# Gated linear attention in smaller tiles of the array: 64x64 score products masked in one pass, output products in column and quarter tiles

## The chip, the cores and the metric

The kernel runs on one core of a Trainium2 chip. The core has five engines, each with its own queue that is worked off in order: TensorE (PE; its weight loads are listed as PEld), VectorE (DVE), ScalarE (ACT), GpSimd (POOL) and SyncE (SP), which issues the DMAs. TensorE multiplies a stationary operand (the weights, up to 128 rows by 128 columns) with a moving operand of up to 512 columns and writes to PSUM, eight banks of 512 f32 values for each of 128 partitions. The metric is the device time of one execution in microseconds (us), lower is better.

## The reference

Two layers over 1024 tokens of width 1024. Each layer projects the normed input to a latent-attention group and to a gated linear attention (GLA) group, multiplies each branch with its gate, projects back, and adds a gated per-layer embedding. The change touches the GLA group: four heads, key width 64, value width 128, chunks of 64 tokens, run forward and backward with separate decays and summed.

```python
def gla_chunked(q, k, v, log_a):          # C = 64, N = S // C = 16 chunks
    b = jnp.cumsum(gc, axis=-2)
    ref = b[..., C // 2 - 1:C // 2, :]
    q_in = qc * jnp.exp(b - ref)
    k_in = kc * jnp.exp(ref - b)
    mask = jnp.tril(jnp.ones((C, C), dtype=bool))
    A = jnp.where(mask, jnp.einsum('nbhid,nbhjd->nbhij', q_in, k_in), 0.0)
    o_intra = jnp.einsum('nbhij,nbhjv->nbhiv', A, vc)
    ...
    def step(state, inp):
        qi, ki, vi, di = inp
        o = jnp.einsum('bhid,bhdv->bhiv', qi, state)
        state = state * di[..., None] + jnp.einsum('bhjd,bhjv->bhdv', ki, vi)
        return state, o
    _, o_inter = lax.scan(step, s0, (q_inter, k_state, vc, decay))
    o = o_intra + o_inter
# o = rmsnorm(gla_chunked(q, k, v, la_f) + flip(gla_chunked(flipped, la_b)), out_norm)
```

## The kernel before

Activations lie transposed, features on the partitions and 1024 tokens along the free axis. Large products split each f32 operand into a high and a low f32r part and add three products (`mm3`, line 162; weights are loaded and split in `load_split`, lines 140 to 142: a DMA, a ScalarE copy, a GpSimd subtraction). The GLA products take f32 operands as they are.

For one GLA head, partitions 0 to 63 hold the key features of the forward direction and 64 to 127 those of the backward one. `gla_decay` (step Z) computes the decays; it begins with a product into a PSUM tile (line 370) and ends with `qi`, `ki` and `qb`. `gla_state` (step S) transposes the keys (line 412), forms the per-chunk state updates (line 425, in two row tiles of 64 rows), copies them out of PSUM (line 104) and runs the scan over the chunks with 28 small VectorE instructions (line 452). It then computes the scores. For each of eight pairs of chunks t, and for each direction, one product of 64 rows takes the 128 tokens of the pair against the same 128 tokens (line 459), so that each product holds four 64x64 blocks, of which the two off the diagonal belong to no chunk. The forward scores go to one PSUM tile and the backward ones to another, each 128x1024. A mask that is zero off the diagonal blocks and triangular in them steers one VectorE pass for each direction (line 461) into `af` and `ab`, which were cleared once a layer; GpSimd adds the two (line 465) to `at`, whose off-diagonal blocks are zero. `gla_out` (step O) adds into one PSUM tile, for each chunk, state times `qb` (line 473: 128x128 weights, 64 moving columns), and for each pair of chunks values times `at` (line 477: 128x128 weights, 128 moving columns). ScalarE copies the result out and squares it (line 480), a norm follows, GpSimd multiplies by the gate, and a DMA writes the head out.

PSUM is held by two tags, `mm` and `aux`, with two buffers of two banks each. Line 370, the state updates, the scores, the output and the norms take `aux`; the big products mostly take `mm`. SBUF tiles of 128x1024 come from one ring of 41 buffers.

The order of the steps is written by hand in two strings, one a layer; within and across steps the program builder orders each engine's queue by a simulation of its own. In layer 0 the string's GLA part reads `K0 R0 Q0 G0+ Z0 V0 K1 S0 Z1 V1 O0 S1 Q1 D0 Z2 G1 G2 P0 O1 S2 ...`: the output of a head comes well after its scores, with other products between.

Of the kernel before, what the change touches and what calls it, by code (L numbers as in the profile page):

```python
# [10 lines left out]
F32 = mybir.dt.float32  # L11
F32R = mybir.dt.float32r
I32 = mybir.dt.int32
U32 = mybir.dt.uint32
AF = mybir.ActivationFunctionType
ALU = mybir.AluOpType
# [3 lines left out]
P = 128  # L20
# [3 lines left out]
HC = 512  # L24
EPS = 1e-6
NH = 4
CH = 64
# [24 lines left out]
ORDER = ("K0 R0 Q0 G0+ Z0 V0 K1 S0 Z1 V1 O0 S1 Q1 D0 Z2 G1 G2 P0 O1 S2 C0 Z3 D1 C1 N0 D2 O2 S3 G3 M0 A0 O3 X0 A1 E0 A2 A3+ H0 k0 T0 s0 v0 H2 k1+ s1 k2 b0 H1 k3 s2 y1 b1 H3+ s3 b2 v1 s4 y0 y3 b3 y2 s5 b4 w0 w1+ s6 w2 b5 w3+ s7 w4 b6 w5+ s8 w6 w7 b7",  # L52
         "Q0 K0 Z0 V0 S0 Z1 V1 S1 Q1 K1 Z2 G0 O0 S2 G1 Z3 G2+ C0 O1 D0 O2 S3 G3 C1 N0 D1 D2+ O3 M0 X0 A0 A1 E0 A2 k0 y2 H0 A3 T0 s0 v0 H3 k1+ s1 H1 b0 H2 s2 k2 b1 s3 y0 k3+ b2 v1 s4 y3 y1 b3 s5 b4 w0 w1+ s6 w2+ b5 w3 s7 w4 b6 w5+ s8 w6+ w7 b7")

ENG = dict(at="P", qi="V", qb="P", og="P", gate="P", sq="V", wlo="P", kT="A", put="A", o="A", ple="A", hadd="V")
TCKW = {"schedule_with_timeline_sim": True}


# [1 line left out]
def hybrid_encoder(ctx: ExitStack, tc: tile.TileContext, xT, pT, pos, vecs, w_in, wq, wk, wv,  # L60
                   wz, w_out, w_gate, w_proj, outT, dbg=None):
    nc = tc.nc
    dbg = dbg or {}

    cp = ctx.enter_context(tc.tile_pool(name="const", bufs=1))
# [13 lines left out]
    ones_r = cp.tile([P, P], F32R, name="ones_r")  # L79
    nc.vector.memset(ones_r.bitcast(F32), 1.0)  # L80

    mask_f = cp.tile([P, P], F32, name="mask_f")
    mask_b = cp.tile([P, P], F32, name="mask_b")
    for m, sgn in ((mask_f, 1), (mask_b, -1)):
        nc.vector.memset(m, 1.0)
        nc.vector.memset(m[0:CH, CH:P], 0.0)
        nc.vector.memset(m[CH:P, 0:CH], 0.0)
        nc.gpsimd.affine_select(out=m, in_=m, pattern=[[sgn, P]], compare_op=ALU.is_ge,
                                fill=0.0, base=0, channel_multiplier=-sgn)
    rmask = cp.tile([P, S], mybir.dt.bfloat16, name="rmask")  # L90
    nc.gpsimd.memset(rmask, 1.0)
    nc.gpsimd.memset(rmask.rearrange("p (n c) -> p n c", c=CH)[:, :, 0:1], 0.0)
# [3 lines left out]
    def bank2(tag="mm"):  # L96
        return pp.tile([P, 2, HC], F32, tag=tag, name="ps")

    def on(site):
        return {"P": nc.gpsimd, "V": nc.vector}[ENG[site]]  # L100

    def copy(site, dst, src):
        if ENG[site] == "A":
            nc.scalar.activation(dst, src, AF.Copy)  # L104
        else:
            nc.vector.tensor_copy(dst, src)
# [7 lines left out]
    def flat(t):  # L114
        return t.rearrange("p a b -> p (a b)")

    def st(shape=(P, S), dt=F32, name="st"):
        return sp.tile(list(shape), dt, tag="st", name=name)

    def mt(dt=F32, name="mt"):  # L120
        return rp.tile([P, S], dt, tag="r", name=name)
# [152 lines left out]
    sq = SquareSum()  # L274
# [8 lines left out]
    for L in range(DEPTH):  # L283
        vb = L * V_LAYER

        def gv(off, j):
            return vec[:, vb + off + j:vb + off + j + 1]
# [5 lines left out]
        rc = cp.tile([P, 8], F32, tag="rc", name="rc", bufs=2)  # L293
        r_x = rstd(sq.acc, D, col=rc)

        af, ab = mt(name="af"), mt(name="ab")
        for t in (af, ab):
            nc.gpsimd.memset(t, 0.0)
        wzr = st(name="wzr")[0:32, 0:HC]
        wzt = mt(F32R, name="wzt")[:, 0:HC]  # L300
        nc.sync.dma_start(wzr, wz[L])
# [104 lines left out]
        def gla_state(h, v, dec):  # L406

            qi, ki, qb, ks_, alpha = dec

            fp = flat(bank2("aux"))  # L410
            for t in range(8):
                nc.tensor.transpose(out=fp[:, t * P:(t + 1) * P], in_=ks_[:, t * P:(t + 1) * P], identity=ident)
            kT = mt(name="kT")
            copy("kT", kT, fp)
            kT = kT.rearrange("p (a b) -> p a b", b=P)

            s0, s1 = (mt(name=n).rearrange("p (n c) -> p n c", c=P) for n in ("s0", "s1"))
            nc.gpsimd.memset(s0[0:CH, 0, :], 0.0)
            nc.gpsimd.memset(s1[CH:P, 7, :], 0.0)
            for half in range(2):  # L420
                pu = bank2("aux")
                for j in range(8):
                    c = half * 8 + j
                    rows = slice((c % 2) * CH, (c % 2) * CH + CH)
                    nc.tensor.matmul(pu[:, j % 2, (j // 2) * P:(j // 2 + 1) * P], lhsT=kT[rows, c // 2, :],
                                     rhs=v[c // 2][rows], start=True, stop=True)

                u4 = pu.rearrange("p b (n c) -> p n b c", c=P)

                def put(dst, src):  # L430
                    copy("put", dst, src)

                if half == 0:
                    put(s0[0:CH, 1:7, :].rearrange("p (n b) c -> p n b c", b=2), u4[0:CH, 0:3])
                    put(s0[0:CH, 7, :], u4[0:CH, 3, 0, :])
                    put(s1[0:CH, 0, :], u4[0:CH, 3, 1, :])
                    put(s0[CH:P, 0, :], u4[CH:P, 0, 1, :])
                    put(s0[CH:P, 1:7, :].rearrange("p (n b) c -> p n b c", b=2), u4[CH:P, 1:4])
                else:
                    put(s1[CH:P, 1:7, :].rearrange("p (n b) c -> p n b c", b=2), u4[CH:P, 1:4])  # L440
                    put(s1[CH:P, 0, :], u4[CH:P, 0, 1, :])
                    put(s0[CH:P, 7, :], u4[CH:P, 0, 0, :])
                    put(s1[0:CH, 1:7, :].rearrange("p (n b) c -> p n b c", b=2), u4[0:CH, 0:3])
                    put(s1[0:CH, 7, :], u4[0:CH, 3, 0, :])

            def state(c):
                return (s0, s1)[c // 8][:, c % 8, :]

            for c in range(1, NCH - 1):
                e = NCH - 1 - c  # L450
                for rows, m, n in ((slice(0, CH), c, c + 1), (slice(CH, P), e, e - 1)):
                    nc.vector.scalar_tensor_tensor(state(n)[rows], state(m)[rows], alpha[rows, m:m + 1],  # L452
                                                   state(n)[rows], op0=ALU.mult, op1=ALU.add)

            blocks = [(af, slice(0, CH), mask_f, flat(bank2("aux"))), (ab, slice(CH, P), mask_b, flat(bank2("aux")))]
            for t in range(8):
                c = slice(t * P, (t + 1) * P)
                for acc, rows, mask, fa in blocks:
                    nc.tensor.matmul(fa[:, c], lhsT=ki[rows, c], rhs=qi[rows, c], start=True, stop=True)
            for acc, rows, mask, fa in blocks:  # L460
                nc.vector.copy_predicated(acc.rearrange("p (n c) -> p n c", c=P),
                                          mask.bitcast(U32).unsqueeze(1).to_broadcast((P, 8, P)),
                                          fa.rearrange("p (n c) -> p n c", c=P))
            at = mt(name="at")
            on("at").tensor_tensor(at, af, ab, op=ALU.add)
            return state, at

        def gla_out(h, v, qb, state, at, gg):

            fo = flat(bank2("aux"))  # L470
            for n in range(NCH):
                cc = slice(n * CH, (n + 1) * CH)
                nc.tensor.matmul(fo[:, cc], lhsT=state(n), rhs=qb[:, cc], start=(n % 8 == 0), stop=False)
                if n % 2:
                    t = n // 2
                    c = slice(t * P, (t + 1) * P)
                    nc.tensor.matmul(fo[:, c], lhsT=v[t], rhs=at[:, c], start=False, stop=(n % 8 == 7))
            o, o2 = mt(name="o"), mt(name="o2")
            copy("o", o, fo)
            nc.scalar.activation(o2, fo, AF.Square)  # L480
            r = rstd(o2, P, tmp=mt)
            nc.vector.scalar_tensor_tensor(o, o, gv(V_ON, 0), r, op0=ALU.mult, op1=ALU.mult)
            on("og").tensor_tensor(o, o, gg, op=ALU.mult)
            nc.sync.dma_start(ygd[h], o)
# [176 lines left out]
        def new_part():  # L661
            return (cp.tile([P, 4], F32, tag="top", name="top", bufs=3),
                    cp.tile([P, 4], F32, tag="sums", name="sums", bufs=4), [])
# [52 lines left out]
        for w in ORDER[L].split():  # L716
            u = int(w[1])
            other[0] = w.endswith("+")
            h, c = divmod(u, 2)
# [6 lines left out]
            elif w[0] == "s":  # L726

                part, halves = new_part(), []
# [24 lines left out]
        sq = SquareSum()  # L753
# [12 lines left out]
        if not last_layer:  # L766
            xs = []
            sq = SquareSum()
# [16 lines left out]
        else:  # L785

            kept = {}
            for w in TAIL:
                n = w.stop - w.start
                k = -(-n // HC)  # L790
                m = n // k
# [5 lines left out]
                acc = mt(name="acc")[:, :n]  # L797
                todo = [t for t in range(8) if t not in kept] + list(kept)
                for at, t in enumerate(todo):
# [4 lines left out]
                    for i in range(8):  # L804
                        for j, (a, b) in enumerate(((ws[i][0], gh[i][0]), (ws[i][1], gh[i][0]),
                                                    (ws[i][0], gh[i][1]))):
                            for c in range(k):
                                nc.tensor.matmul(ps[:, c, :], lhsT=a, rhs=cut(b[:, w])[:, c, :],  # L808
                                                 start=(i == 0 and j == 0), stop=(i == 7 and j == 2))
# [108 lines left out]
```

## Time and profile before

| | |
|---|---|
| median of 3 runs | 1502.29 us (1501.21 to 1503.48) |
| profiled execution | 1500.96 us, span from first to last instruction 1499.2 us |
| granted TensorE clock, mean share of full speed | 0.977 |
| busy: TensorE, VectorE, ScalarE, GpSimd | 94%, 63%, 42%, 40% of the span |
| instructions | 19117 |

Busy times of TensorE's products are modelled and overlap: products follow one another more closely than their lengths. The distance from the start of one group of instructions to the start of the next is the better measure, and the timeline gives it. The granted clock is the share of 2.4 GHz that TensorE was given; 0.5 is 1.2 GHz. A wait is put down to the instruction that released it last.

### The profile page before, as it was taken

Reading aid. Unit: us, or ns where it says so; the run is one execution under the profiler, and the core shown is the slowest. Engines: PE = TensorE matmul, PEld = TensorE weight load, DVE = VectorE, ACT = ScalarE, POOL = GpSimd, SP = SyncE. Lnnn points to the kernel's source line nnn. Section 1 sums busy time; section 2 is a strip of 40 time slices with the busy share of each in tenths; the row PEclk is TensorE's granted clock in tenths of the full one; section 3 lists DMA queues with packets and bytes.
Section 4 is the critical chain, followed back from the end, with each engine's and each line's share of the span. In section 5 each row is a group of like instructions: output and inputs, shape, how many; then the busy total and the mean of one; then the engine's idle time right before and its main releaser. Section 6 shows DMA issues by size and latency. Waiting matters only on the chain. (4 is left out here: it accounts for less than half of the span.)

```text
span 1499.2 us, 19117 instructions
## 1 busy us (share of the span) xinstructions
PE 1415.7 (94%) x7508; PEld 1207.3 (81%) x7508; DVE 942.8 (63%) x1244; ACT 624.7 (42%) x826; POOL 598.6 (40%) x344
## 2 busy tenths in 40 slices
PE   7999899999789999999999999989989999999995
PEld 6799788878678888888889977878777888878994
DVE  2687856788655654465566867775855664447548
ACT  6454364343344443253334434533234544325331
POOL 3643333322264545124543413331335645412564
PEclk9999999999999999999999989999999999999997
DMA  8321123112401021213332121111350021111333
GB/s 283 123 74 54 51 69 141 39 57 84 133 30 56 23 91 50 63 49 113 134 121 73 35 57 50 36 46 43 93 167 29 29 71 50 70 43 57 120 103 122
DMA packets 51289, 117.40 MB, mean 78 GB/s; under 512 B 6592, under 2 KB 11584, under 8 KB 51200
## 3 DMA queue, kind: packets, MB, share of 16 engines
q1 hardware_dynamic: 51200, 116.19, 24.0%
q8 instruction: 59, 0.97, 0.3%
q14 instruction: 30, 0.25, 0.1%
HBM read 82.34 MB, written 25.43 MB: 72 GB/s over the span
## 5 line engine op out<-in xcount | busy, mean ns | idle before, releaser
L142 POOL TENSOR_TENSOR wl<-wr,wh 128x512 fp32r<-128x512 f32 (+2 forms) x184 | 275.4, 1499 | 607.3 <-ACT wh L141 549.7
L141 ACT ACTIVATE wh<-wr 128x512 fp32r<-128x512 f32 (+2 forms) x184 | 111.7, 611 | 346.1 <-PE ps L162 218.9
L658 POOL TENSOR_SCALAR sc<-sc,sums 128x1024 f32<-128x1024 f32 x64 | 181.8, 2850 | 90.7 <-DVE sums L657 76.3
L452 DVE SCALAR_TENSOR_TENSOR s<-s,last 64x128 f32<-64x128 f32 x208 | 90.6, 436 | 32.4 <-ACT s L104 25.4
L129 DVE TENSOR_TENSOR el<-ps,eh 128x1024 fp32r<-128x1024 f32 x64 | 78.0, 1221 | 47.2 <-ACT eh L128 46.4
L656 ACT ACTIVATE sc<-ps,top 128x1024 f32<-128x1024 f32 x64 | 71.4, 1116 | 80.7 <-DVE top L654 76.7
L653 DVE TENSOR_REDUCE top<-ps 128x1 f32<-128x1024 f32 x64 | 78.3, 1223 | 39.5 <-PE ps L650 39.3
L162 PE MATMUL ps<-xh,wh 128*128 128x512 f32 x288 | 92.7, 401 | 5.3 <-DVE gate L358 4.8
L162 PE MATMUL ps<-x0h,wh 128*128 128x512 f32 x288 | 91.6, 400 | 3.9 <-DVE gate L358 3.4
L162 PE MATMUL ps<-xh,wl 128*128 128x512 f32 x288 | 90.7, 396 | 0.0
L162 PE MATMUL ps<-x0l,wh 128*128 128x512 f32 x288 | 90.7, 396 | 0.0
L162 PE MATMUL ps<-xl,wh 128*128 128x512 f32 x288 | 90.6, 394 | 0.0
L162 PE MATMUL ps<-x0h,wl 128*128 128x512 f32 x288 | 90.4, 395 | 0.0
L162 PE MATMUL ps<-yh,wh 128*128 128x512 f32 x256 | 80.7, 392 | 0.9 <-DVE h L710 0.9
L162 PE MATMUL ps<-yl,wh 128*128 128x512 f32 x256 | 79.4, 390 | 0.0
L162 PE MATMUL ps<-yh,wl 128*128 128x512 f32 x256 | 79.3, 390 | 0.0
L128 ACT ACTIVATE eh<-ps 128x1024 fp32r<-128x1024 f32 x64 | 65.3, 1022 | 31.8 <-PE ps L671 30.2
L671 PE MATMUL ps<-ident,sc 128*128 128x128 f32 x512 | 66.2, 273 | 4.6 <-DVE ql L129 3.0
L671 PEld LDWEIGHTS ps<-ident,sc 128*128 128x128 f32 x512 | 59.3, 140 | 13.0 <-DVE ql L129 3.5
L162 PEld LDWEIGHTS ps<-xh,wh 128*128 128x128 f32 x288 | 54.4, 192 | 17.9 <-DVE gate L358 5.3
L162 PEld LDWEIGHTS ps<-x0h,wh 128*128 128x128 f32 x288 | 54.5, 192 | 15.5 <-DVE gate L358 3.5
L162 PEld LDWEIGHTS ps<-x0h,wl 128*128 128x128 f32 x288 | 55.1, 191 | 11.8
(257 smaller groups left out, 3627.3 us busy)
## 6 DMA issues: line engine op xcount, KB each, us to landing
wr<-in_w_in SPq DMA_DIRECT2D x88, 256.0 KB, 2.6
wr<-in_w_gate SPq DMA_DIRECT2D x40, 256.0 KB, 2.6
projd<-po SPq DMA_DIRECT2D x16, 512.0 KB, 3.6
wr<-in_w_out SPq DMA_DIRECT2D x32, 256.0 KB, 2.6
xraw<-in_xT SPq DMA_DIRECT2D x8, 512.0 KB, 4.4
gqk<-gqk SPq DMA_DIRECT2D x16, 256.0 KB, 2.9
ygd<-o SPq DMA_DIRECT2D x8, 512.0 KB, 2.6
gad<-gate SPq DMA_DIRECT2D x8, 512.0 KB, 2.9
```

Source lines behind the costliest of these rows:

```text
L128: nc.scalar.activation(hi, src, AF.Copy)
L129: nc.vector.tensor_tensor(lo, src, hi.bitcast(F32), op=ALU.subtract)
L141: nc.scalar.activation(hi[:, :n], raw[:, :n], AF.Copy)
L142: on("wlo").tensor_tensor(lo[:, :n], raw[:, :n], hi[:, :n].bitcast(F32), op=ALU.subtract)
L162: nc.tensor.matmul(ps[:, c, :], lhsT=a, rhs=b[:, c * HC:(c + 1) * HC], start=(i == 0 and j == 0), stop=(i == n - 1 and j == 2))
L452: nc.vector.scalar_tensor_tensor(state(n)[rows], state(m)[rows], alpha[rows, m:m + 1], state(n)[rows], op0=ALU.mult, op1=ALU.add)
L653: nc.vector.tensor_reduce(m, flat(ps), axis=AX.X, op=ALU.max, negate=True)
L656: nc.scalar.activation(e, flat(ps), AF.Exp, bias=m, scale=SCALE, accum_out=sums[:, b:b + 1])
L658: nc.gpsimd.tensor_scalar(e, e, sums[:, b:b + 1], None, op0=ALU.mult)
L671: nc.tensor.transpose(out=ps[:, j, b * P:(b + 1) * P], in_=e[:, kt], identity=ident)
```

## The change

Scores: each direction's product is taken for one chunk alone, 64 rows by 64 weight columns with 64 moving columns, and written to the partition half of the chunk's place in its pair (b) and to the bank of its direction (d). The four combinations of d and b are the four 64x64 tiles of the array. Both directions now lie in one PSUM tile, one bank each. The mask keeps only the 64x64 triangle for each direction, and one pass of 128x1024 masks both directions into one tile `afb`; `at` is their sum over 128x512, now on VectorE.

Output: the state product of a chunk is split in two column tiles of 64 weight columns (w). The value product is split by chunk (row half b) and by value half (w) into four quarter tiles. Even chunks lie in one bank and odd ones in the other; all state products come first, then all value products. The copies out of PSUM write the tokens back in order, in pieces of 64.

```diff
-ENG = dict(at="P", qi="V", qb="P", ...
+ENG = dict(at="V", qi="V", qb="P", ...
...
-    mask_f = cp.tile([P, P], F32, name="mask_f")
-    mask_b = cp.tile([P, P], F32, name="mask_b")
-    for m, sgn in ((mask_f, 1), (mask_b, -1)):
-        nc.vector.memset(m, 1.0)
-        nc.vector.memset(m[0:CH, CH:P], 0.0)
-        nc.vector.memset(m[CH:P, 0:CH], 0.0)
-        nc.gpsimd.affine_select(out=m, in_=m, pattern=[[sgn, P]], compare_op=ALU.is_ge,
+    mask = cp.tile([P, 2, CH], F32, name="mask")
+    wide = cp.tile([P, P], F32, name="wide")
+    for d, sgn in ((0, 1), (1, -1)):
+        nc.vector.memset(wide, 1.0)
+        nc.gpsimd.affine_select(out=wide, in_=wide, pattern=[[sgn, P]], compare_op=ALU.is_ge,
                                 fill=0.0, base=0, channel_multiplier=-sgn)
+        for half in (slice(0, CH), slice(CH, P)):
+            nc.vector.tensor_copy(mask[half, d], wide[half, half])
...
-        af, ab = mt(name="af"), mt(name="ab")
-        for t in (af, ab):
-            nc.gpsimd.memset(t, 0.0)
+        afb = mt(name="afb").rearrange("p (d t c) -> p d t c", d=2, c=CH)
+        nc.gpsimd.memset(afb, 0.0)
...
-            blocks = [(af, slice(0, CH), mask_f, flat(bank2("aux"))), (ab, slice(CH, P), mask_b, flat(bank2("aux")))]
+            fa = bank2("aux")
             for t in range(8):
-                c = slice(t * P, (t + 1) * P)
-                for acc, rows, mask, fa in blocks:
-                    nc.tensor.matmul(fa[:, c], lhsT=ki[rows, c], rhs=qi[rows, c], start=True, stop=True)
-            for acc, rows, mask, fa in blocks:
-                nc.vector.copy_predicated(acc.rearrange("p (n c) -> p n c", c=P),
-                                          mask.bitcast(U32).unsqueeze(1).to_broadcast((P, 8, P)),
-                                          fa.rearrange("p (n c) -> p n c", c=P))
-            at = mt(name="at")
-            on("at").tensor_tensor(at, af, ab, op=ALU.add)
+                for d in range(2):
+                    rows = slice(d * CH, (d + 1) * CH)
+                    for b in range(2):
+                        c = slice((2 * t + b) * CH, (2 * t + b + 1) * CH)
+                        nc.tensor.matmul(fa[b * CH:(b + 1) * CH, d, t * CH:(t + 1) * CH], lhsT=ki[rows, c],
+                                         rhs=qi[rows, c], start=True, stop=True)
+            nc.vector.copy_predicated(afb, mask.bitcast(U32).unsqueeze(2).to_broadcast((P, 2, 8, CH)),
+                                      fa.rearrange("p d (t c) -> p d t c", c=CH))
+            at = mt(name="at")[:, :HC]
+            on("at").tensor_tensor(at.rearrange("p (t c) -> p t c", c=CH), afb[:, 0], afb[:, 1], op=ALU.add)
...
-            fo = flat(bank2("aux"))
+            fo = bank2("aux")
+            halves = (slice(0, CH), slice(CH, P))
             for n in range(NCH):
-                cc = slice(n * CH, (n + 1) * CH)
-                nc.tensor.matmul(fo[:, cc], lhsT=state(n), rhs=qb[:, cc], start=(n % 8 == 0), stop=False)
-                if n % 2:
-                    t = n // 2
-                    c = slice(t * P, (t + 1) * P)
-                    nc.tensor.matmul(fo[:, c], lhsT=v[t], rhs=at[:, c], start=False, stop=(n % 8 == 7))
+                c = slice(n // 2 * CH, (n // 2 + 1) * CH)
+                for w in halves:
+                    nc.tensor.matmul(fo[w, n % 2, c], lhsT=state(n)[:, w], rhs=qb[:, n * CH:(n + 1) * CH],
+                                     start=(n < 2), stop=False)
+            for t in range(8):
+                c = slice(t * CH, (t + 1) * CH)
+                for b, rows in enumerate(halves):
+                    for w in halves:
+                        nc.tensor.matmul(fo[w, b, c], lhsT=v[t][rows, w], rhs=at[rows, c],
+                                         start=False, stop=(t == 7))
+            fo = fo.rearrange("p b (t c) -> p b t c", c=CH)
+            def spread(t):
+                return t.rearrange("p (t b c) -> p b t c", b=2, c=CH)
             o, o2 = mt(name="o"), mt(name="o2")
-            copy("o", o, fo)
-            nc.scalar.activation(o2, fo, AF.Square)
+            copy("o", spread(o), fo)
+            nc.scalar.activation(spread(o2), fo, AF.Square)
```

## Rows read from the trace of the kernel before

**Rows 1.** The page's first part: busy us, share of the span, instructions.
```profile
PE 1415.7 (94%) x7508; PEld 1207.3 (81%) x7508; DVE 942.8 (63%) x1244; ACT 624.7 (42%) x826; POOL 598.6 (40%) x344
```

**Rows 2.** Stretches: us; busy of PE, PEld, DVE, ACT, POOL; clock, DMA, GB/s.
```profile
33.00:403.00 370.00, 351.76 (x1976) 301.28 (x1975) 269.81 (x366) 161.84 (x213) 132.92 (x79) 0.97 0.26 81
761.00:1110.00 349.00, 331.01 (x1881) 283.67 (x1880) 250.47 (x349) 142.65 (x190) 110.93 (x72) 0.97 0.21 65
100.00:160.00 60.00, 60.00 (x439) 55.69 (x439) 45.29 (x58) 26.51 (x39) 26.62 (x17) 1.00 0.17 49
280.00:350.00 70.00, 64.73 (x366) 54.74 (x365) 59.03 (x92) 23.96 (x35) 20.29 (x14) 0.95 0.15 47
```

**Rows 3.** TensorE's waits: for whom; us in total, times, longest.
```profile
PE ps L162 <- DVE gate L358: 10.2, 3, 4.8
PE ps L370 <- DVE af L461: 9.2, 3, 4.2
```

**Rows 4.** Groups by line: scores; busy us, mean ns, idle before.
```profile
L459 PE MATMUL ps<-qi,d 64*128 64x128 f32 x256 | 25.5, 280 | 0.0
```

**Rows 5.** Timeline of TensorE at 248 and 119 us: start, us, instruction, count.
```profile
248.06 0.39 PE L162 MATMUL ps<-x0h,wh 128*128 128x512 f32 x1
248.37 2.05 PE L459 MATMUL ps<-qi,d 64*128 64x128 f32 x16
250.35 0.50 PE L162 MATMUL ps<-x0h,wh 128*128 128x512 f32 x1
...
119.48 2.06 PE L425 MATMUL ps<-gv,kT 64*128 64x128 f32 x32
121.47 0.39 PE L344 MATMUL ps<-wh,x0h 128*128 128x256 f32 x1
```

**Rows 6.** Timeline of TensorE: output products of two heads, at 145 and 883 us.
```profile
145.80 0.56 PE L473 MATMUL ps<-b,s 128*128 128x64 f32 x4
146.19 0.44 PE L477 MATMUL ps<-at,gv 128*128 128x128 f32 x2
146.47 0.56 PE L473 MATMUL ps<-b,s 128*128 128x64 f32 x4
...
151.08 0.70 PE L162 MATMUL ps<-x0h,wh 128*128 128x512 f32 x2
...
883.70 1.11 PE L473 MATMUL ps<-b,s 128*128 128x64 f32 x4 [0.39 <-DVE ab L461]
...
885.14 0.95 PE L473 MATMUL ps<-b,s 128*128 128x64 f32 x4
...
886.42 0.95 PE L473 MATMUL ps<-b,s 128*128 128x64 f32 x4
```

**Rows 7.** Two more stretches, columns as in rows 2.
```profile
883.00:893.30 10.30, 9.91 (x42) 9.12 (x41) 9.63 (x8) 5.52 (x5) 3.58 (x2) 0.50 0.53 129
937.60:941.00 3.40, 3.37 (x7) 2.21 (x8) 2.19 (x2) 2.19 (x3) 2.23 (x1) 0.51 0.00 0
```

**Rows 8.** Timeline at 932 us, VectorE and TensorE; in brackets the idle time before.
```profile
932.40 3.79 DVE L452 SCALAR_TENSOR_TENSOR s<-s,last 64x128 f32<-64x128 f32 x10
936.22 1.29 DVE L461 COPY_PREDICATED af<-mask_f,ps 128x1024 f32<-128x1024 uint32 x1
...
937.56 1.15 PE L370 MATMUL ps<-lr,wzt 96*128 96x512 f32 x2 [4.15 <-DVE af L461]
```

**Rows 9.** Groups by line and shape, columns as in rows 4.
```profile
L461 DVE COPY_PREDICATED af<-mask_f,ps 128x1024 f32<-128x1024 uint32 x8 | 10.4, 1300 | 0.2
L465 POOL TENSOR_TENSOR at<-af,ab 128x1024 f32<-128x1024 f32 x8 | 19.4, 2426 | 87.8 <-DVE ab L461 87.8
L693 DVE TENSOR_TENSOR ym<-ps,oq 128x512 f32<-128x512 f32 x16 | 11.0, 688 | 45.3 <-PE ps L689 40.7 <-DMA wr<-in_w_out 3.1 <-issue 1.5
L104 ACT ACTIVATE s<-ps 64x768 f32<-64x768 f32 x32 | 24.9, 801 | 20.8 <-PE ps L425 20.6
L480 ACT ACTIVATE o<-ps 128x1024 f32<-128x1024 f32 x8 | 8.1, 1018 | 0.0
```

More of the change, by code (lines that the diff above doesn't have):

```diff
@@ L53 @@
          "Q0 K0 Z0 V0 S0 Z1 V1 S1 Q1 K1 Z2 G0 O0 S2 G1 Z3 G2+ C0 O1 D0 O2 S3 G3 C1 N0 D1 D2+ O3 M0 X0 A0 A1 E0 A2 k0 y2 H0 A3 T0 s0 v0 H3 k1+ s1 H1 b0 H2 s2 k2 b1 s3 y0 k3+ b2 v1 s4 y3 y1 b3 s5 b4 w0 w1+ s6 w2+ b5 w3 s7 w4 b6 w5+ s8 w6+ w7 b7")
-ENG = dict(at="P", qi="V", qb="P", og="P", gate="P", sq="V", wlo="P", kT="A", put="A", o="A", ple="A", hadd="V")
+ENG = dict(at="V", qi="V", qb="P", og="P", gate="P", sq="V", wlo="P", kT="A", put="A", o="A", ple="A", hadd="V")
 TCKW = {"schedule_with_timeline_sim": True}
```

## The prediction

> **What bounds the kernel now.** I read the engine shares first: TensorE is busy for 94% of the span and no other engine for more than 63% [rows 1]. Then the stages: the gated linear attention (GLA) runs in two of them, 33 to 403 us (layer 0) and 761 to 1110 us (layer 1). TensorE is idle in them for only 18.2 and 18.0 us, and between 100 and 160 us for nothing, while VectorE has 11 to 15 us of slack in 60 or 70 [rows 2]. So a microsecond of TensorE time that goes in there moves the end, except at the places where TensorE waits already. The list of its waits names them: it waited 9.2 us for the first masking pass (three times, before the decay product of line 370) and 10.2 us for a gate product on VectorE, 4.8 of them at once [rows 3]. The change has therefore to be priced on TensorE first and on VectorE's queue second.
>
> **Scores.** An f32 product shows as two records on TensorE. Before, a head has 16 products of 64x128 weights, 32 records, and all eight heads keep TensorE busy for 25.5 us [rows 4], 3.2 us each. Why it varies shows in the timeline: 16 records of one direction alone take 1.98 us to the next instruction, while 32 records of line 425, which alternates between the upper and lower 64 rows, take 1.99 us [rows 5]. Two row tiles thus overlap; one alone takes one record in about 112 ns. What is left over (1.98 - 16 x 0.112 = 0.19, and an entry 0.08 longer than the 0.23 between its neighbours) is the price of a switch of tile shape, 0.28 us.
>
> After, a head has 32 products, 64 records, of 64x64. The trace holds no tile of 64 columns. The nearest rows are the output products: per block six records take 0.67 us, 112 ns each, and it is the same 112 for 64 moving columns (line 473) as for 128 (line 477) [rows 6]. So the moving side doesn't set it; I take it that the 128 weight columns do. Then a tile of 64 columns takes 56 ns, and with two tiles at once a record costs 28 ns. Bounds: 14 ns if all four tiles run at once, 56 ns if TensorE takes records no faster than the densest stretch shown (32 in 1.79 us). I take 28, the row pair's overlap and half the columns, without a gain from the fourth tile. Scores after: 64 x 0.028 + 0.28 = 2.07 us a head, 16.6 us for eight: **8.9 us less**.
>
> The Trainium skill, TensorE: Matmul & The Clock Gate, section "LDWEIGHTS (loading the stationary operand)", has the load's time scale with the weight's columns and not with its rows. The 112 ns that don't change with the moving columns agree; that 64 columns take half, no row here shows.
>
> **Output.** Before: eight blocks of six records, 145.80 to 151.08 us, 5.28 us a head [rows 6], 42.2 us for eight. After: 32 products in column tiles (128 rows, 64 columns) and 32 in quarter tiles, 128 records. At 28 ns that is 3.58 us, and 0.45 us for one switch more than scores need, 4.03 us a head, 32.2 us: **10.0 us less**. Bounds: column tiles one after the other, 64 x 0.056 + 64 x 0.028 + 0.45 = 5.83 us (4.4 us more for eight heads); quarter tiles four at once, 3.14 us (17.1 us less). One head runs at half the clock: its blocks take 1.28 us in place of 0.67 [rows 6], and the granted share there is 0.50, 1.2 GHz [rows 7]. The same saving is worth about **1 us** more on six such blocks.
>
> **Waits.** The scores held both buffers of the tag `aux`; now they hold one. Before, the product of line 370 needed an `aux` buffer and waited for the masking pass, which stood in VectorE's queue behind ten state updates: 3.79 us of updates from 932.40, masking from 936.22, and line 370 began at 937.56 after 4.15 us of waiting [rows 8]. With a free buffer that wait goes. Two of the three times an output product comes next and needs an `aux` buffer itself (at 883.70 us it waits for the second masking pass [rows 6]), so the wait only moves to it; at 937 us big input products follow. I count 4.2 us, and the half-clock stretch of 3.4 us just after it [rows 7], worth 1.7: **5.9 us**. Between nothing and 9.2 plus that.
>
> **VectorE and GpSimd.** One masking pass of 1.30 us a head goes; its twin stays at 128x1024. The sum `at` leaves GpSimd (2.43 us a head) and comes to VectorE at half the width; the nearest row is a 128x512 sum at 0.69 us [rows 9]. Queued behind it on VectorE are state updates and the gate products, for which TensorE waits. Net 0.6 us a head less in that queue. It counts where TensorE waits for VectorE behind the scores, at three of eight heads, the two whose wait moves to the output and the one of the 4.8 us: **1.8 us**. Were `at` as slow as on GpSimd, this would be 3.4 us lost. GpSimd's queue behind `at` holds weight splits, and it is idle 60% of the span: nothing. The copies of the output now write 64-column pieces. ScalarE already does so for the states, 768 columns in 0.80 us, as many per us as 1024 in 1.02 [rows 9]: nothing; twice the time would be 2 us a head on ScalarE, 42% busy, ahead of the norm. One 128x1024 clear a layer goes and the masks are built with six small VectorE instructions, as before: nothing. No DMA is added or moved.
>
> **Given back.** At those same three heads VectorE's updates set when TensorE goes on, so scores that end sooner only lengthen the wait: 3/8 of 8.9 = **3.3 us**. The builder orders every queue by its own simulation, so orders may come out otherwise; I allow one longest wait either way (4.8 us [rows 3]) and nothing in the middle.
>
> **Sum.** 8.9 + 10.0 + 1 + 5.9 + 1.8 - 3.3 = 24.3 us. The profiled execution took 1500.96 us (span 1499.2); it gives 1476.7. The median shown is 1.33 us above that execution, so I forecast 1478.0.
>
> **Rivals.**
> *All four quarter tiles at once* (14 ns). For: row tiles overlap almost fully. Against: no row has more than two at once. Scores save 16.1, output 17.1; with 3/8 of 16.1 given back, 35.9 us in all: 1466.4 us.
> The Trainium skill, TensorEngine Tiling (Array Packing), section "Performance Considerations", puts about 60 cycles on each matmul and advises against taking the tiling factor from a dimension that is small already. At 2.4 GHz that is an estimate of 25 ns a record, near my 28 and against the 14; the trace shows no record sequence that dense.
>
> *Column tiles in turn* (56 ns for column tiles, 28 for quarters). They share rows, and rows are all the trace shows as overlapping. Output costs 4.4 more, scores save 8.9, the other terms 4.4: 8.9 us less, 1493.4 us.
>
> *TensorE's own pace, the slower side.* The change doubles the records of the scores and takes those of the output from 48 to 128. If 56 ns a record is what TensorE can take at all, output is 128 x 0.056 + 0.45 = 7.62 us (+18.7 for eight) and scores 3.86 us (+5.4); less the 7.7 us of waits and queue that is +16.4: 1518.7 us. It decides from the record cost at which 192 records and 0.73 us equal the old 8.5 us a head and 0.96 of waits: 45 ns. For it: 56 is the densest average shown. Against it: 56 there is a pair in 112, which the tile explains.
>
> *Taken back.* TensorE gets faster and waits for VectorE: no change, about 1501 us. For it the gate waits; against it the stretch of 60 us without any idle time.
>
> **Chances.** Forecast 0.43, four at once 0.12, column tiles in turn 0.22, taken back 0.08, TensorE's pace 0.15. The range from 1462 to 1506 takes in the first four and leaves out the last and a tail of an order gone wrong. What a measurement can tell from no change is about 0.2%, 3 us: faster 0.76, same 0.08, slower 0.16.
>
> **What would show it.** Right: some 64 records of 64x64 in about 2.1 us, 128 of the output in about 4.0 us; TensorE's records up by 896 (56 products of two, eight heads); the wait of line 370's product at most 5 us; one masking pass of 1.3 us a head and `at` on VectorE near 0.7 us. Wrong: a record cost of 45 ns or more; column tiles that start 56 ns apart; new waits of TensorE for the masking pass at the output products of more than 9 us; or new half-clock stretches.

## The result, and the profile after

The changed kernel takes 1483.09 us (median of four runs, 1482.05 to 1483.94) against 1502.84 us for the kernel before on the same chip: ratio 0.9872, 95% interval 0.9861 to 0.9884, 19.75 us faster. The profiled execution took 1483.45 us, its span is 1481.7 us, 17.5 less than the span before.

The first part of its page answers [rows 1]. TensorE lost 27.8 us of busy time and has 896 more records, VectorE lost 13.0 us and GpSimd 25.2.

```profile
PE 1387.9 (94%) x8404; PEld 1173.7 (79%) x8404; DVE 929.8 (63%) x1244; ACT 625.7 (42%) x828; POOL 573.4 (39%) x334
```

The timeline of TensorE (start, us, instruction, count) shows the new products in two places. The 64 records of a head's scores take 1.09 us to the next instruction; the 32 before took 2.53 with both directions together (second fence, from the kernel before), and 16 of one direction 1.98 [rows 5]. An output of 128 records takes 3.11 us, where 48 took 5.28 [rows 6].

```profile
144.63 2.09 PE L477 MATMUL ps<-b,s 128*64 128x64 f32 x64
146.65 1.16 PE L483 MATMUL ps<-at,gv 64*64 64x64 f32 x64
147.74 0.50 PE L162 MATMUL ps<-x0h,wh 128*128 128x512 f32 x1
...
245.42 0.39 PE L162 MATMUL ps<-x0h,wh 128*128 128x512 f32 x1
245.74 1.16 PE L461 MATMUL ps<-qi,d 64*64 64x64 f32 x64
246.83 0.50 PE L162 MATMUL ps<-x0h,wh 128*128 128x512 f32 x1
```

```profile
173.27 2.60 PE L459 MATMUL ps<-qi,d 64*128 64x128 f32 x32
175.80 0.50 PE L162 MATMUL ps<-x0h,wh 128*128 128x512 f32 x1
```

Inside the scores the start times come in fours: 5 to 8 ns apart three times, then a gap, 59 ns from four to four. That is four tiles at once, 14.7 ns a record. The column tiles start in pairs, 58 ns from pair to pair: 29 ns a record.

For what follows I sum the GLA products' TensorE time over all heads: for each record of scores and output the time to the next record's start, at most 0.30 us (0.45 at half clock), so that a wait is not counted. Before it is 72.0 us (scores 24.9, output 47.2), after 37.5 us (8.7 and 28.8). TensorE thus saved **34.5 us**; the span shows 17.5 (51%), the median 19.75 (57%). About half came back. Of the 17.0 us that are missing between the two spans, 10.3 are idle time of TensorE (83.5 us of the span before, 93.8 after, from the shares above and [rows 1]). The other 6.7 are busy time, which fell by 27.8 and not by 34.5; no run splits them further. The mean granted clock hardly moved, 0.975 against 0.977. The stretches of the two GLA stages, the columns as in [rows 2], show where the idle time is: 26.5 and 21.4 us, against 18.2 and 18.0.

```profile
33.00:400.00 367.00, 340.53 (x2429) 286.11 (x2429) 263.54 (x367) 164.36 (x217) 120.03 (x75) 0.96 0.26 83
756.00:1093.00 337.00, 315.65 (x2338) 267.08 (x2337) 246.19 (x349) 142.15 (x190) 100.29 (x69) 0.97 0.21 68
```

TensorE's waits (for whom; us in total, times, longest), which answer to [rows 3], name the places. The product that begins the decays no longer waits for the masking pass; other products now wait for it or for state updates, 13.5 us in all. Before, waits for a masking pass or for `at` came to 11.3 us, the 9.2 of [rows 3] and the last two lines of the second fence, which is the kernel before. The gate waits grew from 10.2 to 12.5, those for a norm (`sqh`) from 5.5 to 9.6.

```profile
PE ps L162 <- DVE gate L357: 12.5, 4, 5.9
PE ps L176 <- ACT sqh L128: 9.6, 3, 4.8
...
PE ps L477 <- DVE s L451: 4.8, 1, 4.8
...
PE ps L162 <- DVE afb L463: 3.2, 1, 3.2
PE ps L477 <- DVE afb L463: 3.1, 1, 3.1
...
PE ps L343 <- DVE afb L463: 2.4, 2, 1.2
```

```profile
PE ps L176 <- ACT sqh L128: 5.5, 3, 2.1
...
PE ps L477 <- POOL at L465: 1.2, 1, 1.2
...
PE ps L473 <- DVE ab L461: 0.9, 2, 0.5
```

The place of [rows 8] in the changed kernel: the masking pass still stands behind the updates in VectorE's queue and begins at 923.70; the big products at 925.05 waited 3.24 us for it. From 923.98 on, after that idle time began, TensorE runs at half the clock (granted share 0.50, 1.2 GHz): the second fence, with the columns of [rows 7].

```profile
920.27 3.40 DVE L451 SCALAR_TENSOR_TENSOR s<-s,last 64x128 f32<-64x128 f32 x9
923.70 1.29 DVE L463 COPY_PREDICATED afb<-mask,ps 128x1024 f32<-128x1024 uint32 x1
...
925.05 1.22 PE L162 MATMUL ps<-xh,wh 128*128 128x512 f32 x2 [3.24 <-DVE afb L463]
...
925.39 0.69 DVE L466 TENSOR_TENSOR at<-afb 128x512 f32<-128x512 f32 x1
```

```profile
923.98:930.81 6.83, 5.76 (x14) 4.52 (x15) 3.19 (x4) 3.53 (x4) 0.00 (x0) 0.50 0.00 0
```

The groups that answer to [rows 4, 9]: one masking pass a head at 1.29 us, and ScalarE's copy with 64-column pieces at the same 1.02 us as before.

```profile
L461 PE MATMUL ps<-qi,d 64*64 64x64 f32 x512 | 9.3, 221 | 0.0
...
L463 DVE COPY_PREDICATED afb<-mask,ps 128x1024 f32<-128x1024 uint32 x8 | 10.3, 1294 | 0.2
...
L492 ACT ACTIVATE o<-ps 128x1024 f32<-128x1024 f32 x8 | 8.1, 1018 | 0.0
```

### The profile page after: what moved, and what is told of

Same layout as the page of the kernel before. It is cut to its first block, busy times and chain, and to the rows that moved or that the text cites. A ratio compares the mean times of both kernels' runs of the same rounds, so it can differ in the third digit from the quotient of the medians.

```text
span 1481.7 us, 20880 instructions
## 1 busy us (share of the span) xinstructions
PE 1387.9 (94%) x8404; PEld 1173.7 (79%) x8404; DVE 929.8 (63%) x1244; ACT 625.7 (42%) x828; POOL 573.4 (39%) x334
## 5 line engine op out<-in xcount | busy, mean ns | idle before, releaser
L142 POOL TENSOR_TENSOR wl<-wr,wh 128x512 fp32r<-128x512 f32 (+2 forms) x184 | 270.3, 1472 | 690.0 <-ACT wh L141 615.8
L129 DVE TENSOR_TENSOR el<-ps,eh 128x1024 fp32r<-128x1024 f32 x64 | 78.0, 1221 | 47.2 <-ACT eh L128 46.4
L451 DVE SCALAR_TENSOR_TENSOR s<-s,last 64x128 f32<-64x128 f32 x208 | 84.6, 407 | 32.6 <-ACT s L104 25.7
```

The lines of the kernel that those rows point to most:

```text
L129: nc.vector.tensor_tensor(lo, src, hi.bitcast(F32), op=ALU.subtract)
L142: on("wlo").tensor_tensor(lo[:, :n], raw[:, :n], hi[:, :n].bitcast(F32), op=ALU.subtract)
```

## The experiments

Theory 1: TensorE got what the fastest of the rivals promised, and half of it came back because VectorE's queue, with 28 state updates of a head ahead of the masking pass and of the gate products, sets when TensorE goes on. Theory 2: the builder laid all queues out anew, and the waits come from an unlucky order, not from VectorE's load. The kernel before ran beside each set (medians 1502.84 to 1503.68 us). The table has the TensorE time of the GLA products, as defined above, and the time.

| kernel | GLA on TensorE, us | time, us | ratio to before, 95% |
|---|---|---|---|
| before | 72.0 | 1502.84 | |
| changed | 37.5 | 1483.09 | 0.9872 [0.9861, 0.9884] |
| tiles one by one | 71.2 | 1496.78 | 0.9954 [0.9939, 0.9969] |
| whole state products | 56.0 | 1495.49 | 0.9947 [0.9932, 0.9962] |
| `at` on GpSimd | 36.6 | 1488.27 | 0.9898 [0.9872, 0.9925] |
| two PSUM buffers | 40.0 | 1498.49 | 0.9975 [0.9966, 0.9985] |
| before, no updates | 66.8 | 1472.71 | 0.9806 [0.9791, 0.9820] |
| changed, no updates | 35.0 | 1448.56 | 0.9640 [0.9625, 0.9654] |
| mask written after the products, before the updates | 37.7 | 1485.41 | 0.9881 [0.9867, 0.9896] |
| mask ahead | 38.6 | 1472.14 | 0.9799 [0.9784, 0.9814] |
| before, mask ahead | 76.7 | 1492.65 | 0.9924 [0.9910, 0.9939] |
| tiles one by one, mask ahead | 73.1 | 1493.40 | 0.9937 [0.9916, 0.9958] |

### Tiles one by one

```diff
-            for t in range(8):
-                for d in range(2):
-                    for b in range(2):
+            for d in range(2):
+                for b in range(2):
+                    for t in range(8):
...
-            for t in range(8):
-                for b, rows in enumerate(halves):
-                    for w in halves:
+            for b, rows in enumerate(halves):
+                for w in halves:
+                    for t in range(8):
```

> The loops over the tiles are turned round: eight products in a row go to the same 64x64 tile, in the scores and in the value products, so no two tiles can work at once; the arithmetic is the same. After the change 64 records took 1.09 us, in groups of four 59 ns apart. If that is four tiles at once, a record now costs about 58 ns: 3.7 us in place of 1.0 at two places a head, 5.4 us a head and 43 us of TensorE time in all. Theory 1 (time saved or added on TensorE is partly made up by its waits for VectorE's queue): 55 to 75% of it shows, 1507 to 1516 us. Theory 2 (the waits came from an unlucky order of the queues and have nothing to do with how long TensorE takes): all of it, about 1526 us. If small records are cheap by themselves and not by overlap: 1483 us.

1496.78 us. The same 64 records in another order take 3.34 us, mostly 58 ns apart:

```profile
249.45 3.40 PE L461 MATMUL ps<-qi,d 64*64 64x64 f32 x64
252.79 0.50 PE L162 MATMUL ps<-x0h,wh 128*128 128x512 f32 x1
```

So without the overlap of the 64x64 tiles nothing of the gain on TensorE is left, although the column tiles of the state products still overlap here. It cost 33.7 us of TensorE time (43 expected; some records still start 4 to 6 ns apart) and 13.7 us of time, 41%, below the range of theory 1 and far below theory 2's "all of it". The traces exclude theory 2 for this pair: VectorE and ScalarE work off their instructions in the same order as in the changed kernel (one of VectorE's 1244 stands elsewhere), so only TensorE's pace differs. The slower TensorE waits less: 2.9 us for masking pass and updates in place of 13.5, 7.8 for the gate in place of 12.5, and its mean granted clock is 0.981 against 0.975.

```profile
PE ps L162 <- DVE gate L357: 7.8, 4, 3.7
...
PE ps L477 <- DVE s L451: 1.9, 1, 1.9
...
PE ps L162 <- DVE afb L463: 1.0, 1, 1.0
```

With as much TensorE time as the kernel before, this one is still 6.7 us faster than that (1503.49 us in its set): that much came from outside the products.

### Whole state products

```diff
-                for w in halves:
-                    nc.tensor.matmul(fo[w, n % 2, c], lhsT=state(n)[:, w], ...
+                nc.tensor.matmul(fo[:, n % 2, c], lhsT=state(n), ...
```

> The state products go back to 128x128 weights, one product a chunk; scores and value products stay as changed. 32 records at 112 ns in place of 64 at 29: 3.6 us in place of 2.0 a head, 12.6 us of TensorE time. These products stand away from the scores' waits, so both theories let most of it through: 1492 to 1496 us. If column tiles did not overlap and only the scores and quarter tiles gained: 1483 us.

1495.49 us, inside the range. 32 records take 3.62 us in place of 64 in 2.02, so column tiles do work in pairs although they share their rows:

```profile
143.01 3.68 PE L476 MATMUL ps<-b,s 128*128 128x64 f32 x32
146.63 1.16 PE L482 MATMUL ps<-at,gv 64*64 64x64 f32 x64
```

On TensorE it cost 18.5 us and not 12.6, part of it at half the clock (granted share 0.50 from 180 to 188 us, where one head's state products lie); 12.4 us of the 18.5 show, 67%.

### The sum on GpSimd

```diff
-ENG = dict(at="V", ...
+ENG = dict(at="P", ...
```

> Only the sum at goes back to GpSimd, at half the width as in the changed kernel. VectorE's queue is 0.69 us a head shorter, at comes 1 us or so later. Theory 1: three or four of the waits of TensorE for VectorE are shorter by 0.7 us, the value products may wait for at once or twice: 1480 to 1485 us. Theory 2: the order of the queues changes again, anything within 5 us of 1483.

1488.27 us, with runs from 1483.22 to 1491.09 and an interval that touches the changed kernel's. It is 3 us above the range: a VectorE queue shorter by 0.69 us a head did not help. TensorE's gate waits are 16.2 us there. Inconclusive for the theories; the move of `at` cost nothing and may have gained a few us.

### Two PSUM buffers for the scores

```diff
-            fa = bank2("aux")
+            fas = [bank2("aux") for d in range(2)]
...
-                        nc.tensor.matmul(fa[b * CH:(b + 1) * CH, d, ...
+                        nc.tensor.matmul(fas[d][b * CH:(b + 1) * CH, 0, ...
-            nc.vector.copy_predicated(afb, ...
+            for d in range(2):
+                nc.vector.copy_predicated(afb[:, d], ...
```

> The scores of the two directions go to two PSUM tiles of tag aux again, and each is masked by its own pass of half the width; everything else as changed. It undoes the freed buffer and costs VectorE about 0.1 us a head. If the freed buffer is worth what the prediction counted (5.9 us): 1488 to 1492 us, with the product that begins the decays waiting for the first masking pass again, 7 us or more in all. If the wait only moved to other products: 1481 to 1486 us.

1498.49 us: 15.4 us of the gain gone, more than either expectation. The wait of the kernel before is back, six times in place of three [rows 3]:

```profile
PE ps L369 <- DVE afb L464: 14.5, 6, 5.0
```

The freed buffer is what lets the next head's decays start; without it 4.5 us are left of the gain. The experiment also splits the masking pass; its two passes take 0.72 us each against one of 1.29, 0.15 us a head, so the second pass alone explains little of the 15.4 us. But TensorE's GLA time is 2.5 us longer here and the queues stand in another order, so the 15.4 us are not the buffer's alone.

### Mask written before the updates

> Scores, masking pass and at are written ahead of the loop of state updates, so that the masking pass stands in VectorE's queue before the 28 updates of its head and not behind them. Theory 1: TensorE's waits for the masking pass (8.7 us in all in the changed kernel) go, the state updates end 2 us later and output products wait for those instead at one or two heads: 1475 to 1480 us, and the half-clock stretches behind these waits become fewer. Theory 2: 1483 us within 4, either way.

1485.41 us, theory 1's gain not seen. But the edit did not do what it was meant to: in the trace VectorE, ScalarE and GpSimd work off every instruction in the order of the changed kernel, most updates still ahead of the masking pass. Why the builder kept that order is not shown. The waits for the masking pass are the same to the tenth, so the run tells nothing of the theories. Its 2.3 us more show how far two sets can lie apart with the same order:

```profile
PE ps L162 <- DVE afb L456: 3.2, 1, 3.2
PE ps L477 <- DVE afb L456: 3.1, 1, 3.1
```

### Mask ahead

The scores, the masking pass and `at` go to the start of the state step, ahead of the transposes, so that VectorE does them before the updates.

```diff
             qi, ki, qb, ks_, alpha = dec
+            fa = bank2("aux")
+            ... scores, masking pass, at
             fp = flat(bank2("aux"))
...
-            fa = bank2("aux")
-            ... scores, masking pass, at
             return state, at
```

> Scores, masking pass and at are written at the start of the state step, ahead of the transposes, so that the masking pass now does stand in VectorE's queue before the updates, in the idle time in which VectorE waits for the states' first copies. Theory 1: the waits for the masking pass (8.7 us) go, those for the gate product get shorter by up to 2 us each, with some half-clock stretches: 1472 to 1479 us. Theory 2: 1483 us within 4, either way.

1472.14 us, 11 us below the changed kernel: the best version here, 0.9799 of the kernel before. The timeline at 906 us shows masking pass and sum 8.8 and 7.5 us ahead of the first update of their head:

```profile
906.48 1.31 DVE L417 COPY_PREDICATED afb<-mask,ps 128x1024 f32<-128x1024 uint32 x1
...
907.82 0.69 DVE L420 TENSOR_TENSOR at<-afb 128x512 f32<-128x512 f32 x1
...
915.29 3.95 DVE L463 SCALAR_TENSOR_TENSOR s<-s,last 64x128 f32<-64x128 f32 x8 [1.30 <-ACT s L104]
```

Its waits have none for the masking pass left among the listed ones, and 1.9 us for the gate. What leads now is of another kind, norms and the embedding's split:

```profile
PE ps L176 <- ACT sqh L128: 12.3, 6, 3.6
...
PE ps L162 <- ACT ph L128: 8.6, 2, 8.3
PE ps L642 <- DVE ql L129: 6.7, 1, 6.7
...
PE ps L162 <- DVE gate L357: 1.9, 1, 1.9
```

### The same move in the kernel before, and with tiles one by one

> The kernel before with its scores, both masking passes and at written at the start of the state step, ahead of the transposes and the updates; products as before. Theory 1 (VectorE's queue, with the updates ahead of the masking passes, makes TensorE wait): the waits for the first masking pass (9.2 us) and part of those for the gate product go here too: 1488 to 1496 us. If the gain of the changed kernel from this move hung on its freed PSUM buffer: 1500 to 1505 us.

1492.65 us, 11 us below its own reference, as theory 1 says: the order cost the kernel before as much as the changed one, and the change did not cause it. It follows that the masking pass's place does not explain what came back of the whole change. With the mask ahead in both kernels the change saves 38.1 us of TensorE time (76.7 to 38.6) and 20.5 us of time, 54%, where 57% showed with the mask behind.

> Mask ahead, and the tiles one after the other as in the first experiment, 33.7 us more TensorE time in the GLA products than with four tiles at once. With the masking pass behind the updates only 13.7 us of that (40%) showed. Theory 1: with that wait gone more of it shows, 60 to 90%: 1492 to 1502 us, against 1472 us with the tiles at once. If the share that shows has nothing to do with the masking pass: about 1486 us.

1493.40 us. 21.3 us of 34.5 us of TensorE time show, 62%, where 41% showed with the masking pass behind the updates. VectorE's order is again the same but for two of 1244 instructions. For the overlap of the tiles alone, the masking pass's place thus changes how much is seen. This kernel has the products' TensorE time of the kernel before with the mask ahead (73.1 and 76.7 us) and its time: with the mask ahead, buffer and single pass are worth nothing more. The 6.7 us that they brought with the mask behind are gone, which is why the whole change gains no more than before.

### Without the state updates

Line 452 (451 after) is left out in both kernels.

> The kernel before with the 28 state updates a head left out (the states stay the single chunks' sums). VectorE loses 98 us of work in all. Theory 1: TensorE waited for VectorE there already, and in the kernel before those waits were some 20 us with the half-clock stretches behind them: 1480 to 1490 us. Theory 2 says nothing of this one by itself.

> The changed kernel with the same updates left out. Theory 1 (the updates in VectorE's queue are what made TensorE wait, and gave back the saved time): without them nearly all of TensorE's 34 us show, so this kernel is 28 to 34 us faster than the kernel before without updates, about 1452 to 1460 us. Theory 2 (order of the queues, not VectorE's load): the difference between the two stays near the 20 us that it is with updates.

1472.71 and 1448.56 us. The kernel before gained 30 us, more than I expected, the changed one 34.5 us. Between the two lie 24.2 us of 31.8 us of TensorE time, 76% for the whole change, where it was 57% with the updates. This is between the theories: more than the 19.75 us with updates, less than the 28 to 34 of theory 1. VectorE's updates explain part of what came back (14.8 us with them, 7.7 without), not all. The queues without updates also stand in another order.

### The embedding projection elsewhere

```diff
-G1 G2 P0 O1 S2 C0 Z3 ... E0 A2 A3+
+G1 G2 O1 S2 P0 C0 Z3 ... E0 A2 A3+        (after S2)
+G1 G2 O1 S2 C0 Z3 ... E0 P0 A2 A3+        (late)
```

Both start from the version with the mask ahead.

> Mask ahead, with the embedding projection of layer 1 (step P0) moved in the order of layer 0 from before O1 to after S2. Its products waited 8.3 us for ScalarE's split of the embedding, which stood behind gate functions. If that wait goes: 1464 to 1470 us. If it is only met at another place: 1470 to 1476 us.

> The same step moved further, to between E0 and A2, where TensorE waited 6.8 us for VectorE's rotary chain at the end of the stage. If its 96 products fill that wait and the 8.3 us go as well: 1460 to 1468 us. If the ring of tiles or ScalarE holds it up there: 1470 to 1478 us.

1474.65 us (0.9802, interval 0.9784 to 0.9820) and 1491.08 us (0.9922, interval 0.9905 to 0.9938). After S2 the 8.3 us wait is gone from the list and the norms' wait is 22.6 us in its place; late, the embedding's wait is 10.4 us and the norms' 19.0. Neither hope held; a wait is met elsewhere, and an order alone can cost 19 us. That much of theory 2 is true, and differences between runs whose queues differ may hold some of it.

```profile
PE ps L176 <- ACT sqh L128: 22.6, 7, 12.0
```

## Why the prediction was right, point by point

The time was forecast at 1478.0 us and is 1483.09. The direction and its reason, products that TensorE finishes faster in two stages that it bounds, held. Two terms of the sum were mis-sized and nearly cancelled: by the profiled executions TensorE saved 14.6 us more than forecast, and 21.4 us more than forecast came back elsewhere. That the time still came out 5.1 us from the forecast is luck.

**Scores and output.** Forecast 8.9 + 10.0 + 1 us less; measured 16.1 and 18.4, 34.5 in all. The step that failed is "I take 28, the row pair's overlap and half the columns, without a gain from the fourth tile": for column tiles 28 was right (29), for quarter tiles the lower bound of 14 was (14.7). The rival with four tiles at once, given a chance of 0.12, had 16.1 and 17.1 us, close to what TensorE saved; its 1466.4 us was wrong by the next term. Half the weight columns do halve the time: one 64x64 tile alone takes a record in 58 ns, where 128 columns took 112. Column tiles in turn (56) and TensorE's own pace (45 or more) are excluded.

The Trainium skill, TensorEngine Tiling (Array Packing), section "Performance Considerations", has about 60 cycles of overhead for each matmul and so nothing to gain from a dimension that is small already. The trace differs: with 64 moving columns, four records in 59 ns. The Trainium skill lists 64x64 as four independent tiles in the section "Overview" of the same page, and the trace agrees: four records in the time that one tile alone takes for one. The Trainium skill, TensorE: Matmul & The Clock Gate, section "LDWEIGHTS (loading the stationary operand)", has the load's time go by the weight's columns; 58 ns for 64 columns against 112 for 128 agree.

**Waits.** Forecast 5.9 us less by the freed buffer, 1.8 by VectorE, 3.3 given back: 4.4 less in all. Measured, by the spans: 34.5 saved and 17.5 seen, 17.0 *more*. The step "with a free buffer that wait goes" was right for its place: line 370's product has no wait for a masking pass in the list. The big products behind it wait for the same masking pass instead, 3.24 us at 925 us. With the tiles one after the other that wait is 1.0 us, so most of it comes of TensorE being there earlier. At that slower pace buffer and single pass, with the new order, brought 6.7 us, near the 5.9 + 1.8 forecast. The step that failed is "Given back ... 3/8 of 8.9", 3.3 us: it reckoned with the scores alone and with three heads. The runs show 20.0 us: of the 33.7 us that the 64x64 tiles' overlap saves, 59% came back in longer waits and a lower clock. With the mask ahead 38% did. For the whole change 43% came back, and 24% without the updates.

**VectorE.** The masking pass that went and `at` at 0.69 us were priced right (row by row 1.29 and 0.69). What they were worth by themselves is not shown; the run with `at` on GpSimd is inconclusive.

**Costs put at nothing.** The copies in 64-column pieces take 1.02 us as before. GpSimd's relief of 25 us shows in TensorE's waits only as the 1.2 us for `at` that are gone.

What stays open: a quarter of the TensorE gain is missing even without updates. Waits explain little of it, for TensorE is idle for 66.9 and 69.0 us in the two spans of 1470.3 and 1444.3 us; its busy time fell by 28.1 us, less than the 31.8 that the GLA products saved. No run shows why.

```profile
PE 1403.4 (95%) x7508; PEld 1198.3 (81%) x7508; DVE 844.0 (57%) x1020; ACT 624.1 (42%) x826; POOL 599.9 (41%) x344
PE 1375.3 (95%) x8404; PEld 1164.4 (81%) x8404; DVE 836.8 (58%) x1020; ACT 626.1 (43%) x828; POOL 584.9 (40%) x334
```

## What to carry to other kernels

Small f32 products are cheap on TensorE when consecutive ones go to different tiles: write the loops so that the tile changes with every product. Price such a gain in two numbers, what TensorE saves and what share can show, and read the share from the waits that stand behind the stretch: here 41% of the tiles' overlap showed with the masking pass behind VectorE's state updates, and 62% with it ahead. An instruction that frees a PSUM buffer belongs ahead of the long chain on its engine: here the scores had to be written ahead of the transposes before the builder ordered it so, and that was worth 11 us in either kernel, over half of what the change gained.

## What the runs showed of the hardware that was not expected

Records of products to the four 64x64 tiles of the array start 5 to 8 ns apart and repeat every 59 ns, with their weight loads; to one tile, in the same kernel with the loops turned round, every 58 ns. Column tiles, which share all rows, overlap too: two records in 58 ns, where those of whole products take 112 ns each.
